# A residual block in fp32 by hi/lo products: x of the second half through DRAM, the second feed-forward product from raw blocks first, its last product by halves of columns

## The chip, the cores and the metric

The kernel runs on one core of one Trainium2 chip. The metric is the device time of one execution in microseconds; less is better. Engines are called by their names: TensorE multiplies matrices, VectorE (DVE in rows) and ScalarE (ACT) work element by element and read the banks (PSUM) that TensorE writes, and SyncE's queue (SP, SPq) issues the transfers between DRAM and the chip's memory. PE stands for TensorE and PEld for its loads of weights.

## The reference

One block over 2048 positions of width 1024, in float32. Its attention and its Mamba-2 mixer aren't touched by the change; what surrounds them is this:

```python
def rmsnorm(x, w):
    return x * rsqrt(mean(x * x, axis=-1) + EPS) * w

hn = rmsnorm(x, norm_mix_w)
q, k, v, z, xbc, dt_raw = split(hn @ w_in)               # 1024 -> 4112 columns
att = chunk_band_attention(q, k, v, rel_bias)            # 512 columns
ssd = ssd_mixer(z, xbc, dt_raw, ...)                     # 1024 columns: conv, scan, gate, norm
h = x + concat([att, ssd]) @ w_out
h = h + square(relu(rmsnorm(h, norm_mlp_w) @ w_ff1)) @ w_ff2    # 1024 -> 4096 -> 1024
y = rmsnorm(h, norm_final_w)
```

## The kernel before

All data lie transposed: features on the 128 partitions, positions along the rows. The positions are worked off in two **halves** of 1024, `s` being the half at work and `n` the next. A half runs through the input projection with the mixer and the attention woven into it (`mixer`), then through `mlp`: the output projection, the first feed-forward product `ff1`, the second `ff2`, and the final norm. Every product is made three times, from a high and a low part of both operands: `split` (L228) has ScalarE round the raw tile to the high part, and VectorE subtract it from the raw tile to give the low part. `mm3` (L245) issues the three matmuls of a term.

**Order.** TensorE's instructions keep the order in which the program writes them. Those of ScalarE, VectorE and SyncE's queue are put into an order by a planner when the kernel is built, from its own model of times; at run time each engine works its list off in order, and a waiting instruction holds up all behind it. `tc.keep_in_program_order` pins an instruction behind the one written before it on its engine. A tile of a pool is handed on to its next user when its last reader is done, by semaphores for each tile.

**Output projection.** `u_wo_y` and `u_wo_a` (L534) add the projections of mixer and attention to x. `u_wo_a` works on pairs of row blocks d: it loads the residual h from `h_d` into `hx` (L546, `stream`: one of two buffers called `strm`), adds the product (L558), derives from it the seven operands `X` of the first product (B11, T1, T2, B22, T3, B21, T4, each as high and low part), and stores h again (L577).

**First product.** `ff1` and `ff2` multiply blocks of 2 x 2 in the Strassen-Winograd manner: seven products P1 to P7 in place of eight. `PA` and `PB` (L48, L49) name the operands: P1, P2 and P4 take raw weight blocks (A11, A12, A22), P5, P6, P7 and P3 take sums of blocks S1 to S4. `ON` (L51) says that P2 accumulates in P1's bank, P3 in P5's and P4 in P7's. `ff1` runs 16 groups `mp` of seven products, in the order `ORD1`. ScalarE copies P1 into `u` (L654), after which P2 may use the bank. The results are squared after a relu and stored to `f_d`, already in the sums that the second product wants. Between groups, `mlp` squares h and sums the squares for the norm (`squares_of`, L1195; groups 0 to 3), makes the norm's factor `s.v` (5) and its rows (6), and, in the first half, does the same for the x of the second half (groups 7 to 12, factor `s.rx`).

**Second product.** `ff2` runs 4 chunks c of seven products, k = 0 to 6, each of 48 matmuls of 512 columns in two groups g of 24. A product loads one operand from `f_d` two products ahead (`load_a`), splits it one product ahead (`split_a`), and likewise sums (`sum_a`, L581) and splits the weights (`split_w`); chunk 0 begins with P5, which takes the sum S1 = A21 + A22. Results gather in `acc` and `accu`. In chunk 1 VectorE adds the residual. In chunk 3, `last_squares` squares each finished block of columns and sums it into `osq`.

**From half to half.** After the second product of the first half (L1255), the kernel loads the raw x of the second half by turns into a `strm` buffer and one of the two weight staging buffers `wraw`; VectorE multiplies by `s.rx`, and both engines split the scaled tile into the high and low `x` tiles, which lie where `ff2` had its tiles (`FREED`, L59, gives the order in which those come free). Then `gm.weave(3)` interleaves the dt projection and the first two convolution columns, so that each x tile is used as it arrives. `last_rows` (L1095) ends the first half: sums of squares by TensorE, a factor for each position by small VectorE operations, a broadcast by TensorE, then for each of two blocks of 512 columns eight multiplications (L1105), each followed by a store. `dt_chain` (L852) turns the dt column into decays by some twenty small dependent operations on VectorE; then the convolutions go on.

**The end.** In the second half `last_rows` follows the last product, for columns 512 to 1023 (n = 1) and then for 0 to 511 (n = 0).

## Time and profile before

| | us |
|---|---|
| median of 3 runs | 2758.28 (2757.67 to 2758.83) |
| the profiled execution | 2756.4 |
| its span, first to last instruction | 2754.7 |
| TensorE busy in it | 2611.8 |
| VectorE busy | 2025.4 |
| ScalarE busy | 1345.1 |

The profile is of one execution. "Busy" counts matmuls by modelled ends, so a busy TensorE may still run at its low clock; the granted clock (PEclk) says whether it does, 1.00 being 2.4 GHz. An idle time before an instruction is given in brackets with what released it, as far as semaphore events show it. Times are counted from the start of the span.

### The profile page before, as it was taken

How to read it: one execution, taken by the hardware profiler on the slowest of the kernel's cores; microseconds unless marked ns; L12 is line 12 of the kernel's file. 1: busy time of each engine (PE TensorE's matmuls, PEld its weight loads, DVE VectorE, ACT ScalarE, POOL GpSimd, SP SyncE). 2: the span in 40 equal slices, each digit the busy share in tenths (PEclk: the TensorE clock that was granted, in tenths of full speed). 3: DMA queues.
4: the chain of work that ended last, by engine and by line, in shares of the span. 5: the costliest groups of instructions: out<-in, count | busy, mean ns of one | idle time of the engine just before them, and what ended most of it. 6: DMA issues, size and time to landing. Idle time of an engine off the chain costs nothing.

```text
span 2754.7 us, 32168 instructions
## 1 busy us (share of the span) xinstructions
PE 2611.8 (95%) x12398; PEld 2138.8 (78%) x12398; DVE 2025.4 (74%) x2842; ACT 1345.1 (49%) x2083; POOL 7.0 (0%) x42
## 2 busy tenths in 40 slices
PE   6999999999899989999679999999999999989997
PEld 4788778788788877888467887787887888878885
DVE  6797777856868666877767877788658777578877
ACT  5565456633556554433326644566335555454332
POOL 0000000000000000000000000000000000000000
PEclk9999999999999999999889999999999999999998
DMA  3232322325545464542232323113245444455432
GB/s 139 82 107 78 106 101 63 125 98 180 197 152 207 152 239 175 192 152 101 100 109 92 108 93 136 47 58 117 91 151 204 163 160 155 169 210 184 160 114 85
DMA packets 124618, 368.37 MB, mean 134 GB/s; under 512 B 10544, under 2 KB 27440, under 8 KB 113968
## 3 DMA queue, kind: packets, MB, share of 16 engines
q1 hardware_dynamic: 124464, 366.32, 37.8%
q8 instruction: 97, 1.59, 0.2%
q14 instruction: 57, 0.47, 0.1%
HBM read 265.48 MB, written 100.79 MB: 133 GB/s over the span
## 4 chain that ended last, share of the span: by engine, by line
PE 80%; DVE 11%; DMA 3%; ACT 3%; issue 2%; SPq 0%; DVEq 0%; ACTq 0%
PE mm L251 25%; PE fb L251 21%; PE mf L251 21%; PE sB L1047 2%; PE mw L251 2%; PE S L1004 2%; PE tp L1029 2%; DMA strm<-h_d 1%; PE yp L954 1%; PE sB L963 1%; PE yp L952 1%; DVE acc L1105 1%; DVE wlo L230 1%; DVE pt L1013 1%; DVE pl L1033 1%
## 5 line engine op out<-in xcount | busy, mean ns | idle before, releaser
L251 PE MATMUL mm<-x,whi 128*128 128x512 f32 x2304 | 747.9, 406 | 10.1 <-ACT u L372 8.2
L251 PEld LDWEIGHTS mm<-x,whi 128*128 128x128 f32 x2304 | 419.4, 190 | 98.0 <-issue 14.6
L251 PE MATMUL mm<-x,wlo 128*128 128x512 f32 x1152 | 454.7, 395 | 0.0
L251 PE MATMUL mf<-ah,w2h 128*128 128x512 f32 x896 | 351.6, 392 | 12.9 <-ACT ah L229 12.9
L251 PE MATMUL mf<-al,w2h 128*128 128x512 f32 x896 | 352.0, 393 | 8.3 <-DVE al L230 8.3
L251 PE MATMUL mf<-ah,wl 128*128 128x512 f32 x896 | 350.9, 392 | 0.0
L251 PEld LDWEIGHTS mm<-x,wlo 128*128 128x128 f32 x1152 | 218.1, 189 | 48.6
L251 PEld LDWEIGHTS mf<-ah,w2h 128*128 128x128 f32 x896 | 169.8, 189 | 49.2 <-ACT ah L229 13.8
L251 PEld LDWEIGHTS mf<-al,w2h 128*128 128x128 f32 x896 | 169.8, 189 | 46.0 <-DVE al L230 11.0
L251 PEld LDWEIGHTS mf<-ah,wl 128*128 128x128 f32 x896 | 169.9, 190 | 35.5
L1015 ACT ACTIVATE pt<-pt,mx 128x640 f32<-128x640 f32 (+4 forms) x128 | 97.5, 762 | 161.9 <-DVE mx L1013 161.3
L229 ACT ACTIVATE ah<-al 128x2048 fp32r<-128x2048 f32 (+1 forms) x58 | 107.0, 1848 | 107.9 <-PE mf L251 105.9
L230 DVE TENSOR_TENSOR wlo<-wraw,whi 128x1024 fp32r<-128x1024 f32 x88 | 107.6, 1223 | 54.8 <-ACT whi L229 50.6
L229 ACT ACTIVATE whi<-wraw 128x1024 fp32r<-128x1024 f32 x88 | 92.7, 1054 | 112.8 <-PE mm L251 91.5
L229 ACT ACTIVATE w<-wraw 128x512 fp32r<-128x512 f32 x128 | 79.7, 628 | 118.6 <-PE fb L251 111.5
L230 DVE TENSOR_TENSOR al<-al,ah 128x2048 fp32r<-128x2048 f32 (+1 forms) x58 | 128.3, 2212 | 12.3 <-ACT ah L229 12.3
L1013 DVE CUSTOM_DVE_ANT_0 pt<-S,bias 128x640 f32<-128x640 f32 (+4 forms) x128 | 94.2, 736 | 31.4 <-PE S L1004 30.9
L787 DVE TENSOR_TENSOR acc<-mf,acc 128x1024 f32<-128x1024 f32 x64 | 77.8, 1220 | 52.2 <-PE mf L251 52.1
L230 DVE TENSOR_TENSOR w<-s,w 128x512 fp32r<-128x512 f32 x96 | 66.1, 688 | 67.0 <-ACT w L229 65.0
L919 ACT ACTIVATE csb<-csb,cst 128x128 f32<-128x128 f32 x256 | 79.3, 389 | 70.9 <-DMA csb<-cs_d 70.0
L229 ACT ACTIVATE w2h<-w 128x1024 fp32r<-128x1024 f32 x64 | 65.3, 1054 | 93.3 <-PE mf L251 79.2
L1033 DVE TENSOR_TENSOR pl<-tp,ph 128x640 fp32r<-128x640 f32 (+4 forms) x128 | 94.0, 735 | 22.2 <-ACT ph L1032 20.8
(295 smaller groups left out, 5302.6 us busy)
## 6 DMA issues: line engine op xcount, KB each, us to landing
f_d<-st SPq DMA_DIRECT2D x32, 1792.0 KB, 6.3
al<-f_d SPq DMA_DIRECT2D x54, 1024.0 KB, 4.8
wraw<-in_win SPq DMA_DIRECT2D x64, 512.0 KB, 3.3
wraw<-in_w SPq DMA_DIRECT2D x64, 512.0 KB, 3.2
w<-in_w SPq DMA_DIRECT2D x28, 1024.0 KB, 4.8
strm<-h_d SPq DMA_DIRECT2D x48, 512.0 KB, 3.8
csb<-cs_d SPq DMA_DIRECT2D x32, 512.0 KB, 4.3
h_d<-strm SPq DMA_DIRECT2D x32, 512.0 KB, 2.7
```

What stands on the lines that cost most here:

```text
L229: act.activation(hi, raw, AF.Copy)
L230: dve.tensor_tensor(lo, raw, hi.bitcast(F), op=ALU.subtract)
L251: pe.matmul(ps, a, b, start=(first and i == 0), stop=(last and i == n - 1), skip_group_check=on)
L787: dve.tensor_tensor(o, b, o, op=ALU.add)
L919: act.activation(E[:, h, :], E[:, h, :], AF.Relu, scale=-1.0, bias=s.cst[:, k:k + 1])
L952: pe.matmul(yo[:, j, :], S[:, bsl(j, P)], Cf[:, ch], start=True, stop=True)
L1004: pe.matmul(S[:, a, 0:w], q[p][hd][:, bsl(lb, P)], s.ks[p][hd][:, k0 + st:k0 + st + w], start=(z == 0), stop=(z == 1))
L1013: dve.tensor_tensor_reduce(out=o_, in0=s_, in1=b_, scale=1.0, scalar=1e30, op0=ALU.add, op1=ALU.min, accum_out=mx)
L1015: act.activation(pt[:, 0:n], pt[:, 0:n], AF.Exp, scale=-1.0, bias=mx, accum_out=sm)
L1029: pe.transpose(tp[:, bsl(c, P)], pt[:, bsl(c, P)], ident)
L1033: dve.tensor_tensor(ol, tp[:, 0:n], oh.bitcast(F), op=ALU.subtract)
L1047: pe.matmul(pv[:, i0 * P:(i1 + 1) * P], lhsT, rhs, start=(z == 0), stop=(z == 2 * len(order) - 1))
```

## The change

- **x through DRAM.** In chunk 0 of the first half's second product, k = 3 to 6, two row blocks of the second half's x each are loaded, scaled by the norm's weight and `s.rx` in one VectorE operation, and stored to a new DRAM tensor `x_d`. At (k, p) = (7, 0), a new step before the last product's results are evacuated, `ff2`'s pool is closed, the x tiles are opened, all eight are loaded from `x_d` into their low parts, and the first four are split; the next two at (7, 1), the last two after the banks are given up. Those evacuations are pinned behind the splits.
- **Weights early.** The two weights of the woven convolutions are loaded at (3, 4) and split at (3, 6); before, one of them was split at (3, 6).
- **The first half's end.** ScalarE copies the broadcast factors from PSUM to `accu`; `dt_chain` begins ahead of the output multiplications, and these are pinned.
- **Second product.** Chunk 0 takes P1, P2, P5, P6, P3, P7, P4 (`ORD2F`), so that it begins with A11 and A12 as they are; loads, banks and first writers follow suit. `FREED` follows the new places of the tiles.
- **Last product.** It is made for all rows before its evacuation (first half), or for columns 0 to 255 and then 256 to 511 (second half). In the second half the rows of n = 1 start before it, the rest of them follows its first 24 matmuls, and n = 0 goes in two parts of 256 columns.
- **Residual tiles.** `hx` of the blocks d = 2, 3, 6 and 7 takes one of two buffers `h` of its own; `s.v` and `s.rx` later take these buffers.
- **Squares later.** The squares of h move from groups 0 to 3 to groups 2 to 5, and the steps behind them by one or two groups.

```diff
+ORD2F = ("P1", "P2", "P5", "P6", "P3", "P7", "P4")
...
+    x_d = dram.tile([NKT, P, TH], F, name="x_d")
...
-                hx = stream(h_d[s.hf, d])
+                if d % 4 < 2:
+                    hx = stream(h_d[s.hf, d])
+                else:
+                    hx = s.vp.tile([P, TH], F, name="hx", tag="h", bufs=2)
+                    sp.dma_start(hx, h_d[s.hf, d])
...
-        order = [(c, p) for c in range(4) for p in (ORD2 if c < 3 else ORD2L)]
+        order = [(c, p) for c in range(4) for p in (ORD2F, ORD2, ORD2, ORD2L)[c]]
...
         for h in (slice(0, 2), slice(2, 4)):
-            load_w(0, "A21", h)
-            load_w(0, "A22", h)
+            load_w(0, "A11", h)
             load_a(0, h)
-        load_w(0, "A11")
-        load_w(0, "A12")
         split_w(0)
         split_a(0)
+        load_w(0, "A12")
         load_a(1)
         yield
+        load_w(0, "A21")
+        load_w(0, "A22")
...
+            if q == len(order) - 1:
+                if s.hf == 0:
+                    banks = [product(g, range(4)) for g in range(2)]
+                    for g in range(2):
+                        yield 3, 7, g
+                        o = s.acc[:, 2 * g:2 * g + 2, 1, 0, :]
+                        tc.keep_in_program_order(dve.tensor_tensor(o, banks[g], o, op=ALU.add))
+                        last_squares(s, g, 1, 0)
+                else:
+                    s.sq = [stream(None, (P, 2, 512), "osq") for _ in range(2)]
+                    for h in range(2):
+                        cs = bsl(h, 256)
+                        for g in range(2):
+                            b = product(g, range(4), cs)
+                            for z in range(2):
+                                o = s.acc[:, 2 * g + z, 1, 0, cs]
+                                dve.tensor_tensor(o, b[:, z, cs], o, op=ALU.add)
+                                act.activation(s.sq[g][:, z, cs], o, AF.Square)
+                            yield 3, 7 + h, g
+                return
...
+        if s.hf == 0:
+            act.activation(s.accu[:, 2 * n, :], r, AF.Copy)
+            r = s.accu[:, 2 * n, :]
+        yield
         for d in range(NKT):
...
-            if mp < 4:
-                for kt in (2 * mp, 2 * mp + 1):
+            if 2 <= mp < 6:
+                for kt in (2 * mp - 4, 2 * mp - 3):
                     squares_of(h_d[s.hf, kt], kt)
...
+            if s.hf == 0 and c == 0 and k > 2:
+                for kt in (2 * k - 6, 2 * k - 5):
+                    hx = stream(xT[kt * P:(kt + 1) * P, TH:2 * TH])
+                    dve.scalar_tensor_tensor(hx, hx, pr[:, C_MIX + kt:C_MIX + kt + 1], s.rx,
+                                             op0=ALU.mult, op1=ALU.mult)
+                    sp.dma_start(x_d[kt], hx)
...
+            if s.hf == 0 and (c, k) == (3, 4):
+                gm.horizon = len(gm.units)
+                gm.load(gm.at + 1)
+                gm.load(gm.at + 2)
             if s.hf == 0 and (c, k) == (3, 6):
-                gm.horizon = len(gm.units)
                 gm.split(gm.at + 1)
+                gm.split(gm.at + 2)
+            if s.hf == 0 and (k, p) == (7, 0):
+                s.es_g.close()
+                n.es_x, n.xp = open_pool("xp1", "left")
+                xt = x_tiles(n)
+                n.xh, n.xl = zip(*(parts(xt[i]) for i in FREED))
+                for hi, lo, src in zip(n.xh, n.xl, (x_d[kt] for kt in range(NKT))):
+                    sp.dma_start(lo.bitcast(F), src)
+                left = list(zip(n.xh, n.xl))
+            if s.hf == 0 and k == 7:
+                for hi, lo in left[4 * p:4 + 2 * p]:
+                    split(hi, lo, lo.bitcast(F))
+            if s.hf == 1 and (c, k) == (3, 6):
+                rows.append(last_rows(s, 1, tail()))
+                next(rows[0])
+            if s.hf == 1 and (c, k, p) == (3, 7, 0):
+                for _ in rows[0]:
+                    pass
+            if s.hf == 1 and (c, k, p) == (3, 8, 0):
+                rows.append(last_rows(s, 0, tail(), 0))
+                next(rows[1])
...
-            for kt in range(NKT):
-                src = xT[kt * P:(kt + 1) * P, TH:2 * TH]
-                xr = w_load(src.rearrange("p (a b) -> p a b", b=P)).rearrange("p a b -> p (a b)") if kt % 2 else stream(src)
-                dve.tensor_tensor(xr, xr, s.rx, op=ALU.mult)
-                split_scaled(xr, pr[:, C_MIX + kt:C_MIX + kt + 1], n.xh[kt], n.xl[kt])
...
             for r in rows:
+                next(r)
+            n.chain = dt_chain(n)
+            next(n.chain)
+            for r in rows:
                 for _ in r:
                     pass
-            n.chain = dt_chain(n)
-            next(n.chain)
```

## Rows read from the trace of the kernel before

**Rows 1.** The page: busy time of the engines, costliest groups (mean ns), transfers.

```profile
PE 2611.8 (95%) x12398; PEld 2138.8 (78%) x12398; DVE 2025.4 (74%) x2842; ACT 1345.1 (49%) x2083; POOL 7.0 (0%) x42
...
L230 DVE TENSOR_TENSOR wlo<-wraw,whi 128x1024 fp32r<-128x1024 f32 x88 | 107.6, 1223 | 54.8 <-ACT whi L229 50.6
L229 ACT ACTIVATE whi<-wraw 128x1024 fp32r<-128x1024 f32 x88 | 92.7, 1054 | 112.8 <-PE mm L251 91.5
...
al<-f_d SPq DMA_DIRECT2D x54, 1024.0 KB, 4.8
```

**Rows 2.** Busy time by stretch: PE, PEld, DVE, ACT, POOL, PE clock, DMA share, GB/s.

```profile
1000.00:1050.00 50.00, 40.73 (x159) 32.33 (x158) 31.99 (x29) 24.03 (x29) 0.00 (x0) 0.86 0.72 273
1050.00:1100.00 50.00, 50.00 (x222) 41.41 (x221) 29.83 (x19) 20.37 (x17) 0.00 (x0) 1.00 0.46 168
1350.00:1400.00 50.00, 32.69 (x145) 24.22 (x146) 22.42 (x35) 12.32 (x13) 0.00 (x0) 0.77 0.30 106
```

**Rows 3.** Stretches of PE, matmuls of `fb` (two rows), then `mf`: busy, clock.

```profile
701.57:725.07 23.50, 16.54 (x59) 0.85 0.54 201
740.00:760.00 20.00, 20.00 (x90) 1.00 0.64 234
...
1045.82:1049.29 3.47, 3.47 (x8) 0.52 0.45 189
```

**Rows 4.** Waits of PE: us in total, times, longest.

```profile
PE fb L251 <- ACT u L654: 8.8, 2, 4.8
...
PE mf L251 <- DVE al L230: 8.3, 6, 2.8
```

**Rows 5.** Timeline of DVE, then ACT, at the end of the output projection.

```profile
691.58 1.23 DVE L558 TENSOR_TENSOR strm<-mf,strm 128x1024 f32<-128x1024 f32 x1 [1.45 <-DMA strm<-h_d]
...
714.72 0.69 DVE L230 TENSOR_TENSOR xT4l<-t,xT4h 128x512 fp32r<-128x512 f32 x1
...
716.87 1.06 ACT L1198 ACTIVATE ra<-strm 128x1024 f32<-128x1024 f32 x1 [2.19 <-DMA strm<-h_d]
...
719.72 0.60 ACT L654 ACTIVATE u<-fb 128x512 f32<-128x512 f32 x1
```

**Rows 6.** Timeline of PE, ACT and DVE where the second product begins.

```profile
1028.47 0.80 PE L251 MATMUL mf<-ah,w2h 128*128 128x512 f32 x1 [6.47 <-ACT ah L229]
...
1045.82 0.80 PE L251 MATMUL mf<-al,w2h 128*128 128x512 f32 x1 [2.14 <-DVE al L230]
...
1026.41 1.06 ACT L229 ACTIVATE w2h<-ws 128x1024 fp32r<-128x1024 f32 x1 [1.89 <-DVE ws L587]
...
1025.16 1.22 DVE L587 TENSOR_TENSOR ws<-w,w 128x1024 f32<-128x1024 f32 x1
```

**Rows 7.** Timeline of PE and DVE from the first half to the second.

```profile
1341.89 0.39 PE L251 MATMUL mf<-ah,wl 128*128 128x512 f32 x1
...
1369.21 1.22 PE L251 MATMUL mw<-x,whi 128*128 128x512 f32 x2 [15.84 <-ACT whi L229]
...
1405.12 5.36 DVE L1105 SCALAR_TENSOR_TENSOR acc<-acc,pr,sB 128x512 f32<-128x512 f32 x8
...
1427.44 0.49 PE L886 MATMUL sB<-at,tri 128*128 128x128 f32 x2 [3.38 <-DVE at L882]
1433.93 1.22 PE L251 MATMUL mm<-x,whi 128*128 128x512 f32 x2 [5.78 <-ACT u L372]
```

**Rows 8.** Timeline of DVE and PE at the end; two matmuls of 256 columns.

```profile
2728.53 1.22 DVE L787 TENSOR_TENSOR acc<-mf,acc 128x1024 f32<-128x1024 f32 x1 [1.81 <-PE mf L251]
...
2734.21 2.08 PE L316 MATMUL mf<-dg,ones 128*128 128x512 f32 x2 [4.03 <-DVE dg L310]
...
2746.09 5.36 DVE L1105 SCALAR_TENSOR_TENSOR acc<-acc,pr,mf 128x512 f32<-128x512 f32 x8 [2.17 <-PE mf L316]
...
641.72 0.28 PE L1047 MATMUL sB<-ph,vt 128*128 128x256 f32 x1
641.83 0.28 PE L1047 MATMUL sB<-pl,vt 128*128 128x256 f32 x1
```

More of the change, by code (lines that the diff above doesn't have):

```diff
@@ L767, in ff2, with product @@
             ah, al = aa[q]
-            for g in range(2):
-                if p not in ON:
-                    bank[p, g] = s.ps.tile([P, 2, 512], F, name="mf", tag=bank_of(c, p), bufs=2)
+            def product(g, js, c=slice(0, 512)):
+                if p not in ON and js[0] == 0 and c.start == 0:
+                    bank[p, g] = s.ps.tile([P, 2, 512], F, name="mf", tag=bank_of(*order[q]), bufs=2)
                 b = bank[ON.get(p, p), g]
                 wh, wl = ws[q][0][g], ws[q][1][:, 2 * g:2 * g + 2, :]
+                for z in range(2):
+                    for _ in mm3(b[:, z, c], [(wh[:, z, bsl(j, P)], wl[:, z, bsl(j, P)], ah[:, j, c], al[:, j, c])
+                                              for j in js], p not in ON and js[0] == 0, js[-1] == 3, p in ON):
+                        pass
+                return b
@@ L773, in ff2 @@
+            for g in range(2):
                 for js in (range(4),) if q else (range(2), range(2, 4)):
-                    for z in range(2):
-                        for _ in mm3(b[:, z, :], [(wh[:, z, bsl(j, P)], wl[:, z, bsl(j, P)], ah[:, j, :], al[:, j, :])
-                                                  for j in js], p not in ON and js[0] == 0, js[-1] == 3, p in ON):
-                            pass
+                    b = product(g, js)
                 dps = slice(2 * g, 2 * g + 2)
@@ L783, in ff2 @@
                     o = s.acc[:, dps, m, n, :]
-                if c == 0 and p not in ("P1", "P7"):
+                if c == 0 and p not in ("P6", "P7"):
                     act.activation(o, b, AF.Copy)
@@ L1153, in mixer @@
             pass
-        s.v = s.vp.tile([P, TH], F, name="v")
         until(s, "woy")
@@ L1217, in mlp @@
                 dve.tensor_tensor(s.rc[:, 0, :], s.rc[:, 1, :], s.rc[:, 1, :], op=ALU.mult)
[L1218 to L1220 removed]
+            elif s.hf == 0 and 8 <= mp < 12:
+                for kt in (2 * mp - 16, 2 * mp - 15):
                     squares_of(xT[kt * P:(kt + 1) * P, TH:2 * TH], kt)
[L1222 to L1223 removed]
+            elif s.hf == 0 and mp == 13:
+                s.rx = s.vp.tile([P, TH], F, name="rx", tag="h", bufs=2)
                 rv = stream(None, name="rv")
@@ L1270, in mlp @@
                 next(products)
+            rows = [last_rows(s, b, n.ps.tile([P, 512], F, name="sB", tag="B", bufs=2)) for b in (1, 0)]
             for r in rows:
@@ L1282, in mlp @@
         else:
-            for b in (1, 0):
-                for _ in last_rows(s, b, tail()):
+            rows.append(last_rows(s, 0, tail(), 1))
+            for r in rows[1:]:
+                next(r)
+            for r in rows[1:]:
+                for _ in r:
                     pass
```

73 lines of the change are left out of this document (38 added, 35 removed).

## The prediction, made before the changed kernel ran

> **What bounds it now.** I read the engine totals first [rows 1]: TensorE is busy for 2611.8 of the 2754.7 us of the span, so all there is to gain is the time in which TensorE waits or runs at its low clock. The table by stretch shows where that is [rows 2]: from 1050 to 1100 us TensorE is full at clock 1.00, while two stretches with a change of stage hold idle time and clocks of 0.86 and 0.77. A dense matmul of 512 columns costs 0.227 us (20 us over 88 starts; the table counts 90 with the two that overlap its edges [rows 3]). At a clock of 0.52, near the lower level of 1.2 GHz, eight take 3.47 us, 0.43 each. Each turn is therefore priced as the time that it took, less the number of its matmuls at 0.227. The waits of TensorE name what came last [rows 4]; the timelines name who stood in front of that.
>
> **A. Output projection to first product (twice).** From 701.57 to 725.07, 23.5 us pass for 59 matmuls [rows 3]; dense they are 13.4, so the turn costs 10.1 us, and as much in the other half. Two causes. VectorE adds the projection to the residual tiles, and these have two buffers: a load waits until the tile two earlier is stored, and VectorE waits for it 1.45 us, one of four such gaps that sum to 4.0 [rows 5]. So the last part of X is finished at 715.4. Then ScalarE, which runs in order, has two squares of the residual ahead of the copy that frees the first bank; they wait for their loads at 716.87, and the copy comes at 719.72 [rows 5]. TensorE waits up to 4.8 us for it [rows 4]. The change gives four of each eight residual tiles two more buffers, and moves the squares two groups on. With the gaps gone X ends near 711.5; 48 matmuls from 701.57 end at 712.5, so both arrive together, and next to be late is VectorE, nearly gapless there. I take 8.5 of 10.1 back, bounds 4 (only the squares' 4.8, less what X still lacks) and 10: **17 us for both halves**. The later squares cost nothing while they hide under 20 us groups; on the path they would be 8 squares and 7 sums of about 1.1 and 1.2 us, 17 us.
>
> **B. First product to second (twice).** TensorE waits 6.47 us at 1028.47, then 2.14 at 1045.82 [rows 6]. ScalarE is free at 1024.52, but its split of the first weights waits 1.89 us for the sum S1 on VectorE, which stands behind the last group's work [rows 6]. With A11 first there is no sum: the split starts at 1024.6, and start and all that follows come 1.8 us sooner. I don't take the whole 6.5: the splits of the new stage stand behind the old stage's last squares in ScalarE's order now, although their data landed long before, and nothing in the change moves them ahead. The second wait is VectorE making S1, S2 and S4 for the first three products; with raw A12 as the second, it has one product less to prepare, so 2.1 to 2.8 us go [rows 4, 6], and in the first half the 1.6 us of low clock behind them. Sum 5.5 and 4.5, **10 us**; bounds 4 (the start alone, in both halves) and 26 (all idle time of these turns and the low clock after it, some 13 us each). What is new: P2 accumulates onto P1's bank right behind it, so its first half waits for a copy of about 1 us by ScalarE; the other half of P1, 24 matmuls or 5.4 us, covers it.
>
> **C. First half to second.** TensorE's last matmul of the second product starts at 1341.89, and the woven input projection runs from 1369.21, after 15.84 us for a split weight [rows 7]: its load stood behind raw x in the two staging buffers. Five matmuls lay between. The change scales x during chunk 0 of the second product, through DRAM; loads it straight into its tiles as these come free; and has both weights split before. Left at the turn are eight splits, 1.05 us on ScalarE and 1.22 on VectorE each [rows 1]. The evacuation of the last product is pinned behind four of the subtractions, and the first matmul of the projection needs its bank. Seven of the eight tiles are free before TensorE ends, so the four subtractions can start when VectorE has done the squares' sums, by my estimate 4 us before TensorE ends, near 1338: 4.9 us, then the evacuation of 1.2, so 1344.5, with the others ahead of use, eight matmuls per tile. From 1369.2, less 1.1 for the five, that is 23.5 us. If none of the four is in place before TensorE ends, four transfers (a load of twice the size takes 4.8 [rows 1], so 10 at most) and the pinned chain of 6 make it 16 later, 1358: 10 us won.
>
> Behind the projection TensorE waits three times more, the last two for 3.38 and 5.78 us [rows 7]. All hang on VectorE: sixteen output multiplications (two such blocks of 5.36), the dt chain that comes after them, from about 1417.0 (1405.12 + 10.7 and a weight's subtraction of 1.2) to 1427.44, and the convolution that frees a buffer before TensorE restarts at 1433.93, 28.7 us after the projection. The change copies the two rows of factors out of PSUM (two copies of about 0.6, as in [rows 5]), so the transposes start about 4 us sooner, and pins the multiplications behind the chain. VectorE's sum stays 10.4 + 10.7 + 4 (three operations of about 1.3) for the convolution: TensorE restarts about 30 us after the projection instead of 28.7. I book **-1.5**: the waits become one. Ends: -5 and +9, the latter if convolutions slip ahead of the multiplications. C is **22 us**, bounds 5 and 32.
>
> The scaling in chunk 0 is 8 operations of about 1.3 us, where VectorE has 20 of 50 us free [rows 2]; 8 loads and 8 stores join the one queue that also loads the second product's operand. I book 0. If the cover failed it would be the rival below.
>
> **D. The end.** Today the last evacuation follows TensorE at 2728.53, the first factors are there at 2734.21, the last eight multiplications (5.36) end at 2751.45, and the last store ends the span 3.2 us later [rows 8]: 26.4 us behind TensorE. The change sends the columns 512 to 1023 out before and during the last product, and splits the rest by 256. It puts onto TensorE's path one row of sums (1.8 us: from TensorE's end, 2728.3, to 2734.21 less the wait of 4.03), a wait of 0.8 for the squares, a broadcast of 1, a wait of about 1.3 for factors that took 4 us, a second row of 12 sums of squares (2.5) and 1.4 of waiting behind output multiplications: TensorE ends 8.8 later. After it come the last evacuations by 256 and sums (2.5), factors (4), broadcast (1), eight half multiplications (3.3) and the store (3): 13.8 instead of 26.4. Net **4 us**, bounds -2 and 8, as every wait between can be one operation of 1.2 longer.
>
> A matmul of 256 columns I price by the pair that starts 0.11 us apart, each with its own weights [rows 8]: 96 of them, 11 us, as long as now.
> The Trainium skill (TensorE: Matmul & The Clock Gate, section LDWEIGHTS) speaks against halving: a load takes 107 ns for 128 columns however few columns are streamed, so taken in series with 256 columns a product by halves would cost 20.7 us and D would end 6 us worse than today. These rows, at 0.11, do not agree with a load in series.
>
> **Sum.** 17 + 10 + 22 + 4 = 53 us. The profiled execution took 2756.4 us (span 2754.7), so 2703.4; the median of the runs, 2758.28, stands 1.9 above it: **2705 us**, 2690 to 2714 if one term misses by its likely error.
>
> **Rivals.**
> - *Operands ready at once* (chance 0.12). In B the splits slip ahead of the last group's squares and TensorE goes from product to product with no idle time: 8 us more per half, 2688. For it: their data landed early. Against it: ScalarE's order, above.
> - *The waits only move* (0.25). VectorE is the bound at C: x's subtractions, evacuation, chain, multiplications and convolutions queue there, and X in A ends no sooner. Then C gives 8 and A 14 to 15: 2722. For it: VectorE's gapless queue behind the projection [rows 7]. Against it: 22.4 of 50 us busy just before [rows 2].
> - *Halved columns cost whole ones* (0.05): 96 times 0.227 instead of 11 us, 2716.
> - *The change is not felt* (0.03), as the order of work in each turn comes out as before: 2757.
> - *Slower* (0.04). In chunk 0 the stores of scaled x wait on the transfer queue for VectorE, and the loads of the second product's operand stand behind them. Such a load is issued two products (21.8 us) ahead and needs 4.8 to land and about 4.4 for both splits [rows 1]: 12.6 us of room. Four products have x on the queue; once each load is over 27 us late, 4 times 14.6 eats all 53 us and the noise. At 30 us: 2775.
>
> **How the numbers follow.** The forecast, 2690 to 2714, has 0.51; its low end overlaps the first rival and its high end the halves. The range runs from the first rival's 2688 with an unexpected 4 at C or D, 2684, to the second's 2722 with 5 more, 2727. The measurement can tell 0.2%, 5.5 us, from no change. Faster: 0.51 + 0.12 + 0.25 + 0.05 = 0.93; same 0.03; slower 0.04.
>
> **What would show it.** A: no wait for the copy into u near 712, and no gap on VectorE for a residual load. B: the first second-product matmul about 4.7 us behind the last first-product one, and no second wait. C: the first projection matmul within 3 us of the last product, weights already split; then one wait of some 15 us on the convolutions' buffer. D: the span ends some 14 us after the last 256-column matmul. The forecast is wrong if the x tiles' loads land only after TensorE has stopped, if VectorE holds the evacuation at the turn back for longer than 6 us, or if matmuls of chunk 0 wait for their operand.

## The result and the profile after

| | us |
|---|---|
| before, median of 4 runs | 2758.56 |
| after, median of 4 runs | 2723.45 (2720.40 to 2724.83) |
| ratio | 0.9867, 95% interval 0.9850 to 0.9885 |
| the profiled execution after | 2723.32, span 2721.6 |

The change is faster by 35 us (33.1 in the two spans) where 53 were forecast; the time lies inside the wide range of 2684 to 2727, near its slow end, and outside the forecast's own 2690 to 2714. Where the 33.1 us come from is read from the same events in both timelines. The lead is the time of before less that of after, and a part of the kernel gains what the lead grows by over it.

| event | before | after | lead |
|---|---|---|---|
| first product, first half, starts | 701.57 | 700.54 | 1.0 |
| its last matmul ends | 1022.00 | 1011.62 | 10.4 |
| second product starts | 1028.47 | 1022.36 | 6.1 |
| its last matmul ends | 1342.28 | 1335.73 | 6.5 |
| woven projection begins in full | 1368.1 | 1343.94 | 24.2 |
| first step of the recurrence | 1492.97 | 1477.65 | 15.3 |
| first product, second half, starts | 2090.88 | 2076.06 | 14.8 |
| its last matmul ends | 2409.25 | 2385.17 | 24.1 |
| second product starts | 2415.73 | 2389.64 | 26.1 |
| its last product but one ends | 2717.4 | 2688.99 | 28.4 |
| end of the span | 2754.7 | 2721.6 | 33.1 |

(1368.1 is 1369.21 of [rows 7] less 1.1 for the five matmuls that ran ahead of it.) Two steps of the lead go down: the turn to the second product in the first half, and the time behind the woven projection.

The waits of TensorE after, by what came last (us in total, times, longest), answer [rows 4]:

```profile
PE mm L253 <- ACT u L374: 24.5, 4, 21.5
PE mf L253 <- ACT ah L231: 15.2, 2, 10.7
...
PE mm L358 <- DVE acc L791: 8.2, 1, 8.2
...
PE mf L253 <- ACT accu L816: 3.6, 1, 3.6
...
PE mf L253 <- DVE al L232: 2.4, 3, 1.3
```

The wait of `fb` for `u` is gone from the list, and that for `al` has shrunk from 8.3 to 2.4. New are one of 21.5 for `u` in the projection and one of 3.6 for `accu`; the two for `ah` are no longer alike, 10.7 in the first half and 4.5 in the second.

The busy time in the stretch that answers [rows 3], 23.5 us from the first `fb` matmul on (the columns of [rows 2]):

```profile
700.54:724.04 23.50, 23.40 (x103) 18.80 (x102) 22.07 (x33) 17.01 (x28) 0.00 (x0) 1.00 0.53 181
```

103 matmuls at clock 1.00 stand where 59 or 60 at 0.85 stood.

The timeline after, of the engines and the transfer queue (SPq) at the three turns of the first half and at the end; it answers [rows 5 to 8]:

```profile
709.75 1.04 ACT L1243 ACTIVATE ra<-strm 128x1024 f32<-128x1024 f32 x1
710.82 0.60 ACT L660 ACTIVATE u<-fb 128x512 f32<-128x512 f32 x1
...
1003.26 6.15 SPq L179 DMA_DIRECT2D strm<-in_xT  x2
...
1010.32 1.28 DVE L1294 SCALAR_TENSOR_TENSOR strm<-strm,pr,rx 128x1024 f32<-128x1024 f32 x1 [6.13 <-DMA strm<-in_xT]
...
1011.63 2.85 SPq L1296 DMA_DIRECT2D x_d<-strm  x2
...
1014.59 0.37 SPq L695 DMA_DIRECT2D w<-in_w  x1
...
1015.90 0.63 ACT L649 ACTIVATE st<-st 128x512 f32<-128x512 f32 x1 [2.37 <-DVE st L677]
...
1022.36 0.80 PE L253 MATMUL mf<-ah,w2h 128*128 128x512 f32 x1 [10.74 <-ACT ah L231]
...
1036.80 2.00 ACT L231 ACTIVATE w2h<-ws 128x1024 fp32r<-128x1024 f32 x2 [5.36 <-DVE ws L593]
...
1038.97 1.94 ACT L816 ACTIVATE accu<-mf 128x1024 f32<-128x1024 f32 x2 [0.17 <-DMA f_d<-st]
...
1040.05 0.50 PE L253 MATMUL mf<-ah,w2h 128*128 128x512 f32 x1 [3.59 <-ACT accu L816]
...
1339.15 2.25 ACT L231 ACTIVATE x<-x 128x1024 fp32r<-128x1024 f32 x2 [3.81 <-DMA x<-x_d]
...
1340.24 2.42 DVE L232 TENSOR_TENSOR x<-x 128x1024 fp32r<-128x1024 f32 x2 [1.20 <-ACT x L231]
...
1342.57 1.22 DVE L791 TENSOR_TENSOR acc<-mf,acc 128x1024 f32<-128x1024 f32 x1
...
1343.94 1.06 PE L358 MATMUL mm<-x,wd 128*48 128x512 f32 x2 [8.21 <-DVE acc L791]
...
1392.98 10.68 DVE L1149 SCALAR_TENSOR_TENSOR acc<-acc,pr,accu 128x512 f32<-128x512 f32 x16
...
1405.45 2.04 ACT L374 ACTIVATE u<-mw 128x512 f32<-128x512 f32 x4
...
1408.65 7.26 DVE L389 SCALAR_TENSOR_TENSOR xs<-u,hcw,xs 128x1024 f32<-128x1024 f32 x6 [3.30 <-ACT xs L386]
...
2713.40 1.22 PE L318 MATMUL mf<-dg,ones 128*128 128x256 f32 x2 [2.94 <-DVE dg L312]
```

(The last of these is the end's one long wait, where [rows 8] have 4.03.) Line 1294 is the scaling of x, written into chunk 0. It runs at 1010.32, ahead of the second product, and VectorE stands 6.13 us for its load, with the results of the last `ff1` group behind it (ScalarE's square of 1015.90 waits for them). The stores of scaled x wait on the queue for VectorE, and the first loads of the second product are issued behind them at 1014.59. At the turn between the halves the evacuation of 1342.57 stands behind splits of x whose loads are late. At 1392.98 the sixteen output multiplications occupy VectorE for 10.7 us, and the copies into `u` and the convolutions come after them.

### The profile page after: what moved, and what is told of

Read it like the earlier page. It is cut to its first block, busy times and chain, and to the rows that moved or that the text cites. A ratio compares the mean times of both kernels' runs of the same rounds, so it can differ in the third digit from the quotient of the medians.

```text
span 2721.6 us, 32403 instructions
## 1 busy us (share of the span) xinstructions
PE 2605.5 (96%) x12480; PEld 2140.3 (79%) x12480; DVE 2023.0 (74%) x2861; ACT 1346.1 (49%) x2092; POOL 6.9 (0%) x42
## 4 chain that ended last, share of the span: by engine, by line
PE 52%; DVE 6%; DMA 2%; ACT 2%; issue 1%; SPq 0%; DVEq 0%; ACTq 0%
PE mf L253 23%; PE mm L253 12%; PE fb L253 11%; PE sB L1078 1%; PE mw L253 1%; PE tp L1060 1%; PE S L1035 1%; DMA f_d<-st 1%; DVE acc L1149 1%; DVE pt L1044 1%; DMA bias<-in_rel 1%; DVE pl L1064 1%; PE yp L985 0%; PE sB L994 0%; PE yp L983 0%
## 5 line engine op out<-in xcount | busy, mean ns | idle before, releaser
L253 PE MATMUL mf<-ah,w2h 128*128 128x512 f32 (+1 forms) x912 | 355.2, 389 | 18.8 <-ACT ah L231 15.2
L253 PE MATMUL mf<-al,w2h 128*128 128x512 f32 (+1 forms) x912 | 354.1, 388 | 2.4 <-DVE al L232 2.4
L253 PE MATMUL mf<-ah,wl 128*128 128x512 f32 (+1 forms) x912 | 353.8, 388 | 0.0
```

Of the source, the lines that this page charges most:

```text
L253: pe.matmul(ps, a, b, start=(first and i == 0), stop=(last and i == n - 1), skip_group_check=on)
```

## The experiments

Each experiment is the kernel after with the edit shown (`...` marks what is left out), and has the name given in brackets. A time is the median of 4 runs unless one run is said; the bracket behind it has the ratio to before and its 95% interval. Kernels of before, on the same chips, took 2758 to 2760 us.

**The scaling of x, pinned and moved.** Pinned into chunk 0 (`pin_scaling`):

```diff
-                    dve.scalar_tensor_tensor(hx, hx, pr[:, C_MIX + kt:C_MIX + kt + 1], s.rx,
-                                             op0=ALU.mult, op1=ALU.mult)
+                    tc.keep_in_program_order(dve.scalar_tensor_tensor(
+                        hx, hx, pr[:, C_MIX + kt:C_MIX + kt + 1], s.rx, op0=ALU.mult, op1=ALU.mult))
```

> The changed kernel with one more condition: each of the eight multiplications that scale x keeps its place in program order on VectorE, behind the work of the second product's first chunk. In the changed kernel they stand earlier: VectorE does six of the eight between 989.3 and 1014.1 us, under the last group of the first product, and waits 6.13 us there for a load of x; the stores of scaled x wait for VectorE on the transfer queue, and the loads of the second product's first operands are issued behind them, from 1014.59 us on. Theory A (the scaling slipped ahead of its place, and that made the turn to the second product in the first half 10.7 + 3.6 us of waiting): the first wait falls to about 4.5 us, what it is in the second half, where x is not scaled, the second wait to under 1 us; with what follows 9 us less, about 2714. Rival B (the new order of products is at fault, P2 on P1's bank and the splits of the raw blocks): the first wait stays near 10 and the second near 3.6 us, 2722 to 2724. Rival C (the scaling now takes the queue and VectorE away from chunk 0): both waits fall, but TensorE waits for operands between 1050 and 1090 us instead, 2720 or more.

2716.59 us (ratio 0.9844, 0.9829 to 0.9860). The waits of TensorE from 1010 to 1335 us:

```profile
PE mf L253 <- ACT ah L231: 4.5, 1, 4.5
PE mf L253 <- DVE al L232: 3.9, 2, 2.9
PE mf L253 <- DVE wl L232: 0.6, 1, 0.6
```

The turn itself mends as theory A has it, and the wait for `accu` goes, so B falls. New waits for operands, 2.9 us at 1123.66 and 0.6 at 1124.80, over 30 us behind where rival C put them, take part of it back. From the end of the first product to the end of the second the kernel is 4.9 us better than after. The other place, chunk 2 (`scale_chunk2`):

```diff
-            if s.hf == 0 and c == 0 and k > 2:
+            if s.hf == 0 and c == 2 and k > 2:
```

> The changed kernel, but the eight scalings of x stand two chunks later in the program: in the second half of chunk 2 of the second product, behind the tiles of the same two buffers that chunk 1 uses for the residual, so they can't slip ahead. With the multiplications pinned into chunk 0, the turn to the second product lost 14.8 us of waiting and kept 5.4, but 3.5 us of new waits for operands with a stretch at clock 0.97 came at about 1100 us, and the time fell by 7 us only. Theory A (chunk 0 and the turn before it have no room on VectorE and the queue, chunk 2 has): the turn keeps 4.5 + 1 us and no wait appears between 1050 and 1330 us: 2711 to 2714. Rival B (the scaling costs some 5 us wherever it stands): 3 us or more of waits for operands move to between 1200 and 1330 us: 2716 to 2720.

2712.95 us (0.9834, 0.9819 to 0.9848). In the same stretch:

```profile
PE mf L253 <- ACT ah L231: 4.5, 1, 4.5
PE mf L253 <- DVE al L232: 0.9, 1, 0.9
```

That is all TensorE waits there; over the stretch the kernel is 10.7 us better than after. Theory A holds: where the scaling ran cost the first half's turn 10.7 us, and what had been booked at nothing does cost nothing two chunks later.

**x loads ahead of the later weights.** `w_load` gets a flag that pins its transfer, set for the fourth and fifth weight (`x_first`; the flag's own lines are left out):

```diff
-            products = gm.weave(3)
+            products = gm.weave(3, True)
```

> The changed kernel, but the loads of the fourth and fifth weight of the next half's projection keep their place in program order on the transfer queue, so the eight loads of scaled x stand ahead of them. In the changed kernel those two wait 23 us together on the queue for a staging buffer, and the first x load is issued only at 1328.07 us, 7.7 us before TensorE ends. Theory A (the x tiles land late because of the queue): the first x load is issued near 1310 to 1320 us, the four splits that stand ahead of the evacuation are through by about 1338, and TensorE's wait of 8.21 us at 1343.94 falls to about 3: 5 us less, 2718. Rival B (the x tiles themselves come free too late, so the loads wait for TensorE wherever they stand): the fourth x load still lands after 1338 and the wait stays above 6 us, 2721 to 2724. The two weights are split later, and at worst that costs a wait of 1 to 3 us at the end of the woven projection.

2722.49 us (0.9871, 0.9855 to 0.9888), TensorE's wait 8.25 instead of 8.21. The queue's issues of x, from timelines of short stretches, and ScalarE's third split:

```profile
1303.23 0.37 SPq L1315 DMA_DIRECT2D x<-x_d  x1
...
1324.57 0.32 SPq L1315 DMA_DIRECT2D x<-x_d  x1
...
1335.45 0.79 SPq L1315 DMA_DIRECT2D x<-x_d  x2
...
1338.94 1.06 ACT L231 ACTIVATE x<-x 128x1024 fp32r<-128x1024 f32 x1 [7.23 <-DMA x<-x_d]
```

The first load is issued at 1303, but between the second and the third the queue waits for TensorE, which reads the third tile's place until its end: its last matmul ends at 1335.65. Theory A falls, B stands. In this order of the tiles two can be in place in time, whatever else the queue carries, and the splits ahead of the evacuation are four. The other five loads follow by 1337.73 without a wait of their own; as the queue works in order, no run shows whether their places were free sooner, and an order with the third tile's place last was not run.

**The evacuation ahead of the splits.** First ahead of all eight (`evac_first`), then behind two (`two_then_evac`):

```diff
-            if s.hf == 0 and k == 7:
-                for hi, lo in left[4 * p:4 + 2 * p]:
-                    split(hi, lo, lo.bitcast(F))
...
-            for hi, lo in left[6:]:
+            for hi, lo in left:
```

> The changed kernel, but all eight splits of x come behind the evacuation of the last product, where the change has six of them ahead of or between it. The loads are left where they are. Theory A (the bank that the projection needs is held up behind splits that wait for late loads): the wait for the evacuation goes, the first projection matmul starts when one x tile is split, 2 to 4 us sooner than in the changed kernel (1340 to 1342 us); behind it TensorE may wait some 1 to 3 us for the last tiles, whose loads land until 1347: 2719 to 2722. Rival B (the splits were the right thing to do first): the projection starts no sooner than 1343.9 and meets its tiles later, 2724 to 2728.

2720.37 us (0.9858, 0.9843 to 0.9873). The start of the projection:

```profile
1338.66 0.66 PE L358 MATMUL mm<-x,wd 128*48 128x512 f32 x1 [4.32 <-ACT x L231]
1340.11 0.66 PE L358 MATMUL mm<-x,wd 128*48 128x512 f32 x1 [0.79 <-DVE x L232]
```

5.1 us of waiting in place of 8.2, and up to the recurrence the kernel is 2.6 us better than after. The medians are 3.1 apart, the size that theory A gave, but their intervals overlap; it is the stage that speaks for A.

```diff
-            if s.hf == 0 and k == 7:
-                for hi, lo in left[4 * p:4 + 2 * p]:
+            if s.hf == 0 and (k, p) == (7, 0):
+                for hi, lo in left[:2]:
...
-            for hi, lo in left[6:]:
-                split(hi, lo, lo.bitcast(F))
+            for hi, lo in left[2:]:
+                act.activation(hi, lo.bitcast(F), AF.Copy)
+                tc.keep_in_program_order(dve.tensor_tensor(lo, lo.bitcast(F), hi.bitcast(F), op=ALU.subtract))
```

> The changed kernel with the first two x tiles split ahead of the last evacuations, and the other six pinned behind them on VectorE. What the two earlier runs show: with the x loads first on the queue, two land by 1330 us and the third only at 1338.9, as the transfer waits for TensorE's last reads of that place, whoever stands in front of it; and with all splits behind the evacuation TensorE waits 4.3 + 0.8 us for the first x tile. Theory A (two of the eight are free in time, six are not): TensorE waits only for the evacuation, about 2 us behind its last matmul, and the sixteen matmuls of the first two tiles cover the third: 5 to 7 us less than the changed kernel, 2717. Rival B (the third tile is late even so): a second wait of 2 us or more follows within the next 8 us: 2719 to 2722.

2729.54 us (0.9895, 0.9880 to 0.9910), slower than either theory. At the turn, then in the second half's first product:

```profile
1340.26 0.92 PE L358 MATMUL mm<-x,wd 128*48 128x512 f32 x2 [4.59 <-DVE acc L791]
...
1348.80 0.43 PE L358 MATMUL mm<-x,wd 128*48 128x512 f32 x1 [2.89 <-DVE x L1339]
...
2111.57 0.57 PE L253 MATMUL fb<-xB22h,w 128*128 128x512 f32 x1 [3.06 <-DVE st L664]
```

The first wait is 3.6 us shorter and the second, which rival B names, takes 2.9 back; up to the recurrence 1.4 us are left of it. The rest of the difference lies in stages that the edit does not touch. In the first product of the second half the build put squares of the residual and results of a group in another order, and TensorE waits 3.1 us there and loses 1.6 more (4.7 in that product, at a mean clock of 0.99 where after has 1.00); at the end the clock is lower as well (last section). `late_output` and `conv_first` show the same other order. So totals are compared below only with the part that each edit reaches.

**What stands in front of the convolutions.** The output multiplications made short (`short_output`):

```diff
-            op = dve.scalar_tensor_tensor(o, o, pr[:, C_FIN + d:C_FIN + d + 1], r, op0=ALU.mult, op1=ALU.mult)
+            if s.hf == 0:
+                o8, r8 = o[:, :8], r[:, :8]
+            else:
+                o8, r8 = o, r
+            op = dve.scalar_tensor_tensor(o8, o8, pr[:, C_FIN + d:C_FIN + d + 1], r8, op0=ALU.mult, op1=ALU.mult)
```

> The changed kernel, but each of the sixteen output multiplications of the first half takes 8 columns instead of 512 (the others of this half are stored unscaled); order and stores are as in the changed kernel. It prices what the multiplications alone hold up. Theory A (they stand in front of the convolutions on VectorE, 16 times 0.66 us, and TensorE's wait hangs on VectorE's sum): the block takes about 2.6 us instead of 10.7, and the wait of 21.53 us falls by 8, to about 13.5; the time by as much, 2715. Rival B (the wait hangs on the stores, which must have left their place before the convolutions' buffers may be written): it stays at 19 or more.

One run, 2715.57 us.

```profile
1407.98 1.22 PE L253 MATMUL mm<-x,whi 128*128 128x512 f32 x2 [13.13 <-ACT u L374]
```

The wait is 8.4 us shorter: VectorE's sum, not the stores. Then the convolutions ahead of the dt chain and the multiplications (`late_output`; the same lines go from `mixer`, and a small tile moves to another pool):

```diff
...
+            n.es_s1, n.sa = open_pool("ssda1", "left")
+            gm.limit = marks[1, "m0"]
+            gm.release()
             n.chain = dt_chain(n)
             next(n.chain)
+            gm.fill(DT1B)
             for r in rows:
                 for _ in r:
                     pass
```

> The changed kernel, but the buffers of the convolutions are opened ahead of the dt chain and the sixteen output multiplications of the first half (a small tile of the factors moves to another pool for it), so that the first two convolutions and the third's projection are written ahead of both. In the changed kernel TensorE waits 21.53 us for a copy into u that ScalarE makes behind two rows: the dt chain on VectorE (1383.6 to 1393.0 us) and the multiplications (1393.0 to 1403.6). Theory A (the convolutions wait only for their turn on VectorE and ScalarE): the copies into u come right behind the projection, TensorE's wait falls to 3 us or less, and the chain and the multiplications hide under the next products: 18 to 20 us less, 2704 to 2706. Rival B (the chain or the stores are needed just as soon, so the wait moves on): a wait of 10 us or more appears in the next 60 us behind it, for the cumulative sums or the first step of the recurrence: 2712 to 2718. Rival C (VectorE's own sum bounds the stretch): the wait stays above 15 us, 2718 to 2724.

2731.30 us (0.9901, 0.9886 to 0.9915).

```profile
1392.49 7.36 DVE L1151 SCALAR_TENSOR_TENSOR acc<-acc,pr,accu 128x512 f32<-128x512 f32 x11
...
1402.31 3.39 DVE L1151 SCALAR_TENSOR_TENSOR acc<-acc,pr,accu 128x512 f32<-128x512 f32 x5
...
1417.81 0.29 DVE L913 TENSOR_TENSOR at<-dtt,nega 128x128 f32<-128x128 f32 x1
...
1418.25 0.76 PE L917 MATMUL sB<-at,tri 128*128 128x128 f32 x2 [18.88 <-DVE at L913]
```

Rival B has the mechanism, not the size. The copies into `u` were early, but the multiplications slipped into the gaps of the chain, whose end moved from 1393 to 1418, and TensorE's next work but one product needs that end. Up to the recurrence this is 2.7 us worse than after; 5.5 more are lost in the second half's first product. So the third try keeps the multiplications pinned behind the chain, and gives TensorE two products before the chain's sums (`conv_first`; pool and small tile as in `late_output`):

```diff
...
+            n.es_s1, n.sa = open_pool("ssda1", "left")
+            gm.limit = marks[1, "m0"]
+            gm.release()
             n.chain = dt_chain(n)
...
-DT1, DT1B, DT2 = 32000, 10000, 5000
+DT1, DT1B, DT2 = 32000, 20000, 5000
```

> The changed kernel with three edits at the start of the second half: the buffers of the convolutions are opened and the first two convolutions are written ahead of the dt chain; the output multiplications stay pinned right behind the chain; and TensorE does two products of the projection instead of one before it asks for the chain's sums (20000 for DT1B). With late_output, TensorE waited 18.88 us for the dt chain in place of the 21.53 for the copy into u: its next instruction but one was the sum over the chain, and VectorE had 10 us of convolutions and 10.7 of multiplications in between. Theory A (VectorE owes about 32 us here, and only TensorE's work in front of the first thing that needs it can hide that): with 21 us of products in front, TensorE waits about 3.5 us for the transposed dt, then under 8 us in all until 1480: 10 us or more less, 2708 to 2713. Rival B (the stretch is bound whatever stands in front): the waits between 1380 and 1480 us still sum to 18 or more, 2719 to 2726.

2713.91 us (0.9840, 0.9824 to 0.9857). TensorE's waits from 1376 to 1480 us:

```profile
PE sB L889 <- DVE dtr L363: 3.5, 1, 3.5
PE sB L928 <- DVE cst L920: 2.7, 1, 2.7
PE mm L253 <- ACT u L374: 1.9, 1, 1.9
```

8.1 us in place of 23.9 (21.53, 0.35 and 2.03): theory A. Up to the recurrence it is 13.8 us better than after, and 2.7 are lost again in the second half's first product, as above. From `late_output` it differs in two things, the place of the multiplications and the second product in front of the sums, and no run has one of them alone.

**The residual tiles.** The extra buffers undone (`no_extra_buffers`), then the squares moved back (`squares_early`):

```diff
-                if d % 4 < 2:
-                    hx = stream(h_d[s.hf, d])
-                else:
-                    hx = s.vp.tile([P, TH], F, name="hx", tag="h", bufs=2)
-                    sp.dma_start(hx, h_d[s.hf, d])
+                hx = stream(h_d[s.hf, d])
```

> The changed kernel without the extra two buffers: all eight residual tiles of each half go through the two streaming buffers again; the squares of the residual stay two groups later in the program. In the changed kernel TensorE passes the turn from the output projection to the first product without a wait in both halves (from 700 to 725 us it starts 110 matmuls, 67 before). Theory A (the residual tiles' two buffers made the whole turn): the waits come back, 1.9 for X and 4 to 5 for the copy into u, about 10 us in each half: 2741 to 2744. Rival B (the squares that stood ahead of that copy made the larger part, and they have moved): only the waits for X come back, 2 to 3 us in each half: 2728 to 2731.

2742.92 us (0.9938, 0.9922 to 0.9955), 19.5 more than after:

```profile
711.65 0.50 PE L253 MATMUL fb<-xT2l,w 128*128 128x512 f32 x1 [1.65 <-DVE xT2l L232]
...
717.17 1.06 ACT L1239 ACTIVATE strm<-strm 128x1024 f32<-128x1024 f32 x1 [0.35 <-DMA strm<-h_d]
718.25 0.60 ACT L656 ACTIVATE u<-fb 128x512 f32<-128x512 f32 x1
...
718.90 0.80 PE L253 MATMUL fb<-xB21h,w 128*128 128x512 f32 x1 [4.46 <-ACT u L656]
```

The first products take 9.0 and 9.1 us longer than in after. The copy into `u` stands behind squares that wait for their loads again, though the squares are still written two groups later.

```diff
-            if 2 <= mp < 6:
-                for kt in (2 * mp - 4, 2 * mp - 3):
+            if mp < 4:
+                for kt in (2 * mp, 2 * mp + 1):
...
-            elif mp == 6:
+            elif mp == 5:
...
-            elif mp == 7:
+            elif mp == 6:
```

> The changed kernel with the residual's squares, their means and the columns of factors two groups earlier again, as in the kernel before; the extra buffers stay. Theory A (the extra buffers alone do it; ScalarE keeps the order of squares and copies that it has in the changed kernel, where two squares still stand ahead of the copy into u at 710.82 us): no wait near 711, the same 110 matmuls from 700 to 725 us, 2722 to 2726. Rival B (the squares' place matters): a wait of 2 to 5 us for the copy into u comes back in each half, 2728 to 2733.

One run, 2725.64 us, 109 matmuls from 700 to 725 us and no wait. Theory A in both: the buffers alone make the turn. Where the squares are written changes nothing here, as the build puts two of them ahead of that copy either way; what counts is whether their loads are late.

**The end.** Whole columns again (`whole_columns`):

```diff
-                if s.hf == 0:
+                if True:
                     banks = [product(g, range(4)) for g in range(2)]
...
-            rows.append(last_rows(s, 0, tail(), 1))
+            rows.append(last_rows(s, 0, tail()))
```

> The changed kernel, but the last product of the second half runs over its 512 columns at once, and with it the squares, factors and output of columns 0 to 511; columns 512 to 1023 still go out ahead of it, as the change has them. Theory A (halving pays by the output that it hides): TensorE saves some 1.7 us of product (48 matmuls at 0.227 instead of 96 at 0.131 a half) and about 5 us of sums, broadcast and waits inside the product, but behind the last matmul come two evacuations, squares, sums, factors of about 4 us, eight whole multiplications (5.4) and the store: about 19 us instead of 14.1, and the time is 2 us less to 3 us more than the changed kernel's, 2721 to 2726. Rival B (the whole gain at the end comes from the halves): 5 us or more later, 2728 to 2731.

2734.52 us (0.9907, 0.9893 to 0.9922), 11 us later than after and later than both theories.

```profile
2700.35 1.02 PE L318 MATMUL mf<-dg,ones 128*128 128x512 f32 x2
...
2701.41 5.35 DVE L1149 SCALAR_TENSOR_TENSOR acc<-acc,pr,mf 128x512 f32<-128x512 f32 x8 [8.45 <-PE mf L318]
2706.69 1.21 DVE L791 TENSOR_TENSOR acc<-mf,acc 128x1024 f32<-128x1024 f32 x1
```

My estimate of 19 us behind the last matmul became 30.0 (2700.52 to 2730.5). From the last product but one to the end it takes 43.5 us, against 37.3 before and 32.6 after. These 10.9 us do not price the halves alone. The branch that the edit switches to is the first half's: it writes the matmuls of both groups before the first evacuation, and it pins the evacuations. So the broadcast for columns 512 to 1023, which after has behind the first 24 matmuls (2695.04), stands behind the whole product here. VectorE waits 8.45 us for it, and the last evacuation, pinned behind the eight early multiplications, starts 6.2 us after the last matmul ends. By that row some 6 of the 10.9 us are that order's, an estimate. Whole columns with the broadcast at its earlier place and free evacuations were not run, so what the halves are worth stays open.

**Three edits together** (`all_mended`). `scale_chunk2`, `two_then_evac` and `conv_first` (with 22000).

> The changed kernel with three edits together: x scaled in chunk 2 of the second product (scale_chunk2), two x tiles split ahead of the last evacuations and six pinned behind (two_then_evac), and the convolutions ahead of the dt chain with two products in front of the chain's sums (conv_first, here with 22000 for DT1B). By their turns alone they gave 10.7, 3.6 and about 15 us. Theory A (each turn hangs on its own queue, so they add up): 2694 to 2698. Rival B (VectorE behind the projection gives part back as the projection starts sooner, or the order of the first product in the second half shifts as it did in two_then_evac, where TensorE lost 3.1 us of wait and some 2 of low clock at about 2100): 2699 to 2706.

2696.10 us (0.9767, 0.9752 to 0.9781), theory A. TensorE's waits, among them:

```profile
PE mf L253 <- ACT ah L231: 8.9, 2, 4.5
...
PE mm L358 <- DVE acc L791: 4.7, 1, 4.7
```

From the end of the first product to the end of the second, the first half now gains 7.4 us on before, and from there to the recurrence 24.2. It beats both kernels: 27 us under after.

## Why the prediction was right or wrong

**Sign and range** were right, the range by its slow rival: the forecast's own 2690 to 2714 was meant for one term that misses, and three missed, all to the slow side, by 22.5 us together. Of the six numbers in the sum of 53, A, the second half's B and D held:

| term | forecast | measured (lead) | what it came to with the order mended |
|---|---|---|---|
| A, both halves | 17 | 9.3 + 9.3 = 18.6 | |
| B, first half | 5.5 | -3.8 | 7.4 |
| B, second half | 4.5 | 2.0 + 2.3 = 4.3 | |
| C, start of the projection | 23.5 | 24.2 - 6.5 = 17.7 | |
| C, behind it | -1.5 | 15.3 - 24.2 = -8.9 | 24.2 for all of C |
| D | 4 | 33.1 - 28.4 = 4.7 | |

The measured terms sum to 32.6; with 1.0 of lead from before the first turn and 0.5 lost between recurrence and first product they make the 33.1.

**A** was right in size, and half right in cause. The extra buffers end X early, as worked out. The last operand, T4, is done on VectorE at 711.59 where 711.5 was worked out. Moving the squares had no part in the result: in the profile after a square still ends right before the copy into `u` (709.75, 710.82), with its load landed early, and `squares_early` changes nothing.

**B, first half**, failed at the step "The scaling in chunk 0 ... I book 0". I took a line's place in the program for its place in time, though ScalarE, VectorE and the queue follow the build's order. The scaling ran under the last `ff1` group. The mechanism that I gave the rival *Slower* (stores of x waiting on the queue for VectorE, operands behind them) is what happened, at the turn and once, not in chunk 0 and four times. The wait for `accu`, which I called covered by 24 matmuls, came from the same delay: ScalarE's copy stood behind a split that waited for late weights (1036.80). With the scaling out of the way (`scale_chunk2`) neither the wait of 10.7 nor that for `accu` is there. In the second half, where x is not scaled, B gave 4.3: its first wait is 4.47 where 4.7 was forecast, and no wait of the kind of 2.14 follows.

**C, the start**: the step that failed is "Seven of the eight tiles are free before TensorE ends". The queue of `x_first` shows two that are free in time for a load to land, and the third 0.2 us before the end. Whether the five behind it on the queue were free sooner isn't shown. As the evacuation was pinned behind four subtractions, the projection waited for the fourth tile: 8.2 us where 2.6 were worked out (1344.5 against 1341.89 of [rows 7]), and 16 at the bound (1358). Two of the prediction's signs of being wrong came: all loads of x but two landed after TensorE had stopped, and the evacuation started 6.8 us behind it (1335.73 to 1342.57), over the 6. Of this the pin's part is about 3 us (`evac_first`); the rest, which hangs on splits and ScalarE's squares in turn, was not taken apart.

**C, behind it**, was mis-sized: -1.5 was booked, with ends of -5 and +9, and -8.9 came, beyond the lower end. One wait stands in place of three, as worked out, but TensorE restarted 33.8 us after the projection (1382.57 to 1416.34), not 30. VectorE's sum of 25.1 came near: the chain took 9.4 us for 10.4 and the multiplications 10.7, but ahead of the restart came six operations of the convolutions, 7.3 us, and not three. The step from 25.1 to 30 named no work. What stood there was 1.0 us before the chain, and 5.0 between the multiplications and the convolutions (1403.66 to 1408.65): the copies of the decays, a weight's subtraction, ScalarE's copies into `u` that come only after them (1405.45), and its first step of the convolution. The later restart is 5.1 of the 8.9 us. The sum had no term for the rest: the projection took 1.5 us longer, at a clock of 0.90 where before had 0.93, and from the restart to the recurrence 2.3 more went (61.3 us for 59.0, clock 0.94 for 0.96). That most of these 21 us of VectorE could have been hidden, `conv_first` showed.

**D** was right: 14.1 us from the last 256-column matmul to the end where 13.8 were worked out. These matmuls start 0.12 us apart (2704.55 to 2707.18 for 23 of them), and the 96 took 12.2 where I took 11. Whether the early output pays without the halves, no run shows (`whole_columns` changed the order as well).
The Trainium skill (TensorE: Matmul & The Clock Gate, section LDWEIGHTS) gives a load of weights its columns divided by 1.2, so 107 ns for 128 columns; taken in series with 256 columns that would be some 0.21 us a matmul, an estimate. Starts 0.12 us apart at clock 1.00 do not agree with a series.

**The rivals.** "The waits only move" had 2722, and the time is 2723.45; its C of 8 is what C gave (8.8), by VectorE's queue as it said. Its other half, that X ends no sooner, was wrong, and the loss that filled its place was B's. So the total agrees with it by two errors of opposite sign. *Operands ready at once*, *Halved columns* and *The change is not felt* did not occur; of *Slower* the mechanism did, once, at the size of B.

## What to carry over

Where a build orders the engines' work, don't book a step that is "written into" a busy stage at nothing until something holds it there: look at which buffers and waits would keep it from running earlier, in front of work that matters, and on which queue its stores will wait. When two blocks of work stand before the same engine's next need, moving one behind the other can move the wait (`late_output`); the gain came when more of TensorE's own work stood in front of the first thing that needs either (`conv_first`). And compare stage by stage by the lead: edits here changed the order of a stage 700 us away and moved the total by as much as their own effect.

## What the hardware showed beside that

The same work at the end, after the same waits of 1.29 and 0.61 us, ran at different granted clocks in two kernels: TensorE's stretches with sixteen sums and 24 matmuls of 256 columns, in after, then in `two_then_evac` (busy, clock, DMA share, GB/s):

```profile
2689.60:2694.50 4.90, 4.89 (x40) 1.00 0.02 3
...
2704.30:2707.50 3.20, 3.20 (x27) 1.00 0.02 5
```

```profile
2692.65:2699.00 6.35, 6.35 (x41) 0.73 0.01 3
...
2708.10:2712.70 4.60, 4.60 (x27) 0.63 0.02 4
```

A mean of 0.63 lies between the two levels, 1.2 and 2.4 GHz. In both kernels TensorE ran the same instructions at 1.00 before; the two stretches, 1.45 and 1.4 us longer, are 2.9 us of the second kernel's time. Why the clock fell in one and not in the other stays open.
